# Samples read as the last 128 of 288 columns: full tiles for norms and transposes, and last squares summed in PSUM

## The chip, the cores and the metric

The kernel runs on one core of a Trainium2 chip. The metric is the device time of one execution in microseconds, as the median of several runs. Inputs lie in the chip's memory, in float32, and so do the outputs.

## The reference, cut to what matters

One inference step of a two-layer decoder over a prompt of 512 tokens and 8 samples of 8 tokens each, with 1024 features: a recurrent layer (with an FFN), one shared key/value projection, an attention layer (with an FFN) and a last norm.

```python
def rms_norm(x, g):
    y = xf * lax.rsqrt(jnp.mean(xf * xf, axis=-1, keepdims=True) + EPS)
    return y * g

for l in range(DEPTH):                                   # 2
    h = modulate(rms_norm(x, norm_g[l, 0]), sh1, sc1)
    if l < N_A_LAYERS:  out = recurrent_block(h, ...)
    else:               out = sliding_sink_attention(q, k_all, v_all, ...) @ attn_w_o
    x = x + g1 * out
    h = modulate(rms_norm(x, norm_g[l, 1]), sh2, sc2)
    x = x + g2 * swiglu(h, ffn_w_in[l], ffn_w_out[l])
    if l == 0:
        kv = modulate(rms_norm(x, kv_norm_g), kv_shift, kv_scale) @ w_kv   # k is rotated
y = rms_norm(x, final_g)
```

The outputs are y for prompt and samples, states of the recurrent layer, and the windows of keys and values with the new ones at their end (`sample_k`, `sample_v`, `prompt_k`, `prompt_v`).

## The kernel before

**Layout.** Tokens are split into two halves h = 0 and 1. A half has 288 columns (`HC`): 256 of the prompt (`HP`) and 32 of four samples. `x[h]` holds the residual stream as 128 features by 8 chunks (`KC`) by 288 tokens, so features lie on partitions and tokens along the free axis. A product of a layer is a chain of matmuls with 128x128 weights and 288 columns moving. Every operand is split into a high and a low part, so each weight block takes three matmuls.

**Order.** The code calls `T` (PE), `V` (DVE), `S` (ACT), `G` (POOL) and `Q` (SP, which issues DMAs); these only record operations, all at line 447 of the profile. A planner (`Recorder.schedule`) then lays all operations out by priority (the place where they were recorded, less what `early(n)` takes off), by estimated costs and by free buffers, and each engine runs its own list in that order. A changed number of operations or buffers therefore moves others too.

**Norms.** While a layer's last product is drained, `residual` adds each chunk to x and `square` adds its square to `acc[h]`. `stats` sums `acc` over the features with matmuls that have `acc` as weights and a column of ones moving: one for each block of tokens in `TOK`, 128, 128 and 32 of them, so that each token's sum lies on a partition. A DVE operation scales them, and `spread` takes the power -1/2 on POOL and turns the columns back into a row that is repeated on all partitions, by three PE transposes; the third has 32 rows. This happens for both halves at three places in the middle (two `norm_f`, one `after_ffn0`) and, spread alone, twice at the start (`x_half`).

**Attention.** `evac_v` transposes the new values (their 32 sample columns into 32 rows) and writes them out; `attn_sample` attends over cache and new tokens, `pn` being the 32 rows of probabilities for the new ones, and `k_out` transposes the new sample keys, once for each of two head groups and each half.

**The last stage.** `out` walks over the chunks m of the last product, all of half 0 ahead of half 1. For each it calls `residual` and `final_chunk`, which transposes the chunk of x back to tokens on partitions (128, 128 and 32 rows) and multiplies by the final gain. After m = 7 comes `final_norm`: square of chunk 7 into its own buffer, sums of `acc` and of that square, three scalings, three powers, then each of three row blocks is scaled in two parts (DVE and ACT) and written by two DMAs.

In profile rows, `mm` and `ada` are PSUM banks, `wh` weight parts, `h` the high and low operands or, in the last stage, the output rows, `small` the column of ones, `ident` the identity, `tst` the columns of sums, and `sl`, `ta`, `tb`, `td` work buffers.

Of the kernel before, what the change touches and what calls it, by code (L numbers as in the profile page):

```python
# [473 lines left out]
def trunk_kernel(ctx, tc, a):  # L474
# [702 lines left out]
    def ffn(l, g, after):  # L1177
# [173 lines left out]
        def out(k, m, h):  # L1351
# [6 lines left out]
            residual(h, o, m, g, last)  # L1358
# [129 lines left out]
    def evac_v(gp):  # L1488
        def f(h, o):
# [6 lines left out]
            T.transpose(t[0:32, 2 * P : 3 * P], u.f[:, HP:HC], ident[:])  # L1496
# [7 lines left out]
            V.tensor_copy(vs[h][0:32, gs], t[0:32, 2 * P : 3 * P])  # L1504
            for b in range(4):
                Q.dma_start(
                    a["sample_v"][4 * h + b, P - NT : P].rearrange("t g d -> t (g d)")[:, gs],
                    vs[h][b * NT : (b + 1) * NT, gs],
# [137 lines left out]
    def attn_sample(bl):  # L1646
        def run(h):
# [17 lines left out]
            pn = KT[1].f[0:32, 0:512].rearrange("p (g b n) -> p g b n", g=2, b=4)  # L1665
# [15 lines left out]
            def second():  # L1681
                t = aux()
                T.transpose(t[:, 0:P], e.f[:, 0:P], ident[:])
                T.transpose(t[0:32, P : 2 * P], e.f[:, P:W], ident[:])
# [3 lines left out]
                V.tensor_copy(pn[:, :, bl, :], t[0:32, P : 2 * P].rearrange("p (g n) -> p g n", g=2))  # L1688
# [8 lines left out]
                for gp in range(2):  # L1697
                    T.matmul(av[:, 256 * gp : 256 * gp + 256], vs[h][0:32, gp * P : (gp + 1) * P], pn[:, gp].rearrange("p b n -> p (b n)"), start=False, stop=True, skip_group_check=True)
# [26 lines left out]

    def k_out(h):
        for gp in range(2):
            t = aux()
            T.transpose(t[0:32, 0:P], A["nk"][:, gp, h, :], ident[:])
            ko_ = sl()  # L1730
            ko = ko_.f[0:32, 0:128]
            S.copy(ko, t[0:32, 0:P])
            for b in range(4):
                Q.dma_start(
                    a["sample_k"][4 * h + b, P - NT : P].rearrange("t g d -> t (g d)")[:, gp * P : (gp + 1) * P],
                    ko[b * NT : (b + 1) * NT, :],
                )
            ko_.done()
            if h == 1:
                T.transpose(t[:, P : 2 * P], KT[0].f[:, gp * 512 + 3 * P : gp * 512 + 4 * P], ident[:])  # L1740
                po = A["out"][gp]
                S.copy(po, t[:, P : 2 * P])
                Q.dma_start(a["prompt_k"][0].rearrange("t g d -> t (g d)")[:, gp * P : (gp + 1) * P], po)

# [42 lines left out]
    def final_chunk(h, c):  # L1787
# [10 lines left out]
        for i, n in enumerate((P, P, 32)):  # L1798
            V.tensor_tensor(yt[h][i][0:n, cs], t[0:n, i * P : (i + 1) * P], gfin[0:n, cs], ALU.mult)

    def final_norm(h):

        w = ta()
        S.activation(w.f[:, 0:HC], x[h][:, KC - 1, :], AF.Square)
        pt = [aux()[0 : ts.stop - ts.start, 0:1] for ts in TOK]
        st, rs = tst[h][:, 0:3], tst[h][:, 3:6]
# [3 lines left out]
        w.done()  # L1810
        for t in range(3):
            n = P if t < 2 else 32
            V.tensor_scalar(st[0:n, t : t + 1], pt[t], 1.0 / D, EPS, ALU.mult, ALU.add)
            G.tensor_tensor(rs[0:n, t : t + 1], st[0:n, t : t + 1], mhalf[0:n, 0:1], ALU.pow)
            for i in range(2):
                cs = slice(512 * i, 512 * i + 512)
                y = yt[h][t][0:n, cs]
                if i:
                    S.activation(y, y, AF.Copy, scale=rs[0:n, t : t + 1])
                else:  # L1820
                    V.tensor_scalar(y, y, rs[0:n, t : t + 1], None, ALU.mult)
                if t < 2:
                    Q.dma_start(a["y_prompt"][0, h * HP + t * P : h * HP + (t + 1) * P, cs], y)
                else:
                    Q.dma_start(a["y_sample"][4 * h : 4 * h + 4].rearrange("b t d -> (b t) d")[:, cs], y)
# [4 lines left out]
    def x_half(h):  # L1830
        st = tst[h]
        for t in ((4, 0, 1), (2, 3))[h]:
# [9 lines left out]
            if t == 4:  # L1842
                V.tensor_scalar(tst[0][0:32, 2:3], y[0:32], 1.0 / D, EPS, ALU.mult, ALU.add)
                V.tensor_scalar(tst[1][32:64, 2:3], y[32:64], 1.0 / D, EPS, ALU.mult, ALU.add)
# [157 lines left out]
```

## Time and profile before

| | |
|---|---|
| runs | 1262.38 us median of 3 (1261.91 to 1264.16) |
| profiled execution | 1263.01 us, of which 1261.2 us are the span of its instructions |
| PE busy | 1237.8 us (98%), 9532 matmul records |
| DVE, ACT, POOL busy | 920.3, 663.1, 252.7 us |
| DMA | 165.38 MB, 131 GB/s over the span |
| chain that ended last | PE 86%, DVE 6%, ACT 4%, DMA 2%, POOL 1% |
| PE in the first 60 us, in 670 to 815 us, in the last 10 us | 49.15, 141.69, 2.52 us busy |

A matmul overlaps the next, so busy time of PE is near the span wherever its instructions follow each other; what one of them costs is seen in the distance between starts or ends of groups. A row of the timeline has its start, its length, engine, operation, `out<-in`, the shape of the weight tile (`128*32` is one with 32 columns, `32*128` one with 32 rows) and how many records it merges; in brackets stands how long the engine was idle before it and what ended that. A row of a group has busy time and mean duration in ns.

### The profile page before, as it was taken

Reading aid. Unit: us, or ns where it says so; the run is one execution under the profiler, and the core shown is the slowest. Engines: PE = TensorE matmul, PEld = TensorE weight load, DVE = VectorE, ACT = ScalarE, POOL = GpSimd, SP = SyncE. Lnnn points to the kernel's source line nnn. Section 1 sums busy time; section 2 is a strip of 40 time slices with the busy share of each in tenths; the row PEclk is TensorE's granted clock in tenths of the full one; section 3 lists DMA queues with packets and bytes.
Section 4 is the critical chain, followed back from the end, with each engine's and each line's share of the span. In section 5 each row is a group of like instructions: output and inputs, shape, how many; then the busy total and the mean of one; then the engine's idle time right before and its main releaser. Section 6 shows DMA issues by size and latency. Waiting matters only on the chain.

```text
span 1261.2 us, 25276 instructions
## 1 busy us (share of the span) xinstructions
PE 1237.8 (98%) x9532; PEld 1166.9 (93%) x9532; DVE 920.3 (73%) x2283; ACT 663.1 (53%) x1498; POOL 252.7 (20%) x542
## 2 busy tenths in 40 slices
PE   7999999999999999999999999999999999999997
PEld 5798999899899899989998997999999999999997
DVE  6998784795577468656778887558957865875776
ACT  4788973764255335514567678538523542552442
POOL 3456351101100010011024335100011011001011
PEclk8999999999999999999999999999999999999999
DMA  9955554535456655464513220332342232332322
GB/s 306 318 179 188 188 177 151 170 86 171 140 152 191 185 167 184 156 194 137 167 33 75 68 60 27 111 97 97 85 133 68 84 110 76 90 100 80 100 69 76
DMA packets 219755, 165.38 MB, mean 131 GB/s; under 512 B 23629, under 2 KB 204841, under 8 KB 219602
## 3 DMA queue, kind: packets, MB, share of 16 engines
q1 hardware_dynamic: 219186, 163.45, 43.0%
q8 instruction: 75, 1.23, 0.4%
q0 software_dynamic: 448, 0.32, 0.1%
q14 instruction: 46, 0.38, 0.1%
HBM read 160.85 MB, written 4.87 MB: 131 GB/s over the span
## 4 chain that ended last, share of the span: by engine, by line
PE 86%; DVE 6%; ACT 4%; DMA 2%; POOL 1%; issue 1%; SPq 0%; ACTq 0%; DVEq 0%
PE mm L447 82%; PE ada L447 4%; DVE wh L447 1%; DVE ta L447 1%; ACT tb L447 1%; DVE sl L447 1%; ACT ta L447 1%; DVE tb L447 1%; ACT h L447 1%; DMA raw<-in_rnn_w_in_dram 1%; ACT wh L447 1%; POOL h L447 1%; DMA reg<-in_ada_w_dram 1%; ACT sl L447 1%; DMA reg<-in_x_prompt_dram 1%
## 5 line engine op out<-in xcount | busy, mean ns | idle before, releaser
L447 PE MATMUL mm<-h,wh 128*128 128x288 f32 x4128 | 596.2, 298 | 3.8 <-ACT h L447 1.8
L447 PEld LDWEIGHTS mm<-h,wh 128*128 128x128 f32 x4128 | 560.5, 188 | 23.2 <-issue 11.3
L447 PE MATMUL mm<-sl,wh 128*128 128x288 f32 x3218 | 460.6, 296 | 0.4 <-ACT sl L447 0.3
L447 ACT CAST wh<-raw 128x512 fp32r<-128x512 f32 (+2 forms) x380 | 269.1, 721 | 345.7 <-PE mm L447 208.9
L447 PEld LDWEIGHTS mm<-sl,wh 128*128 128x128 f32 x3218 | 436.6, 188 | 9.0 <-issue 5.9
L447 DVE TENSOR_TENSOR wh<-raw,wh 128x512 fp32r<-128x512 f32 (+2 forms) x380 | 310.2, 828 | 59.3 <-ACT wh L447 57.0
L447 DVE SCALAR_TENSOR_TENSOR x<-mm,mods,x 128x256 f32<-128x256 f32 x160 | 77.0, 482 | 136.1 <-PE mm L447 136.0
L447 POOL TENSOR_TENSOR td<-td,td 128x288 f32<-128x288 f32 x38 | 35.5, 934 | 475.8 <-ACT td L447 467.7
L447 POOL TENSOR_TENSOR x<-x,ta 128x32 f32<-128x32 f32 x152 | 55.3, 364 | 331.1 <-DVE ta L447 325.9
L447 PE MATMUL mm<-tb,wh 128*128 128x288 f32 (+1 forms) x488 | 88.5, 296 | 0.4 <-ACT td L447 0.4
L447 PEld LDWEIGHTS mm<-tb,wh 128*128 128x128 f32 x488 | 72.4, 188 | 1.9 <-DVE sl L447 0.8
L447 ACT COPY td<-mm 128x288 f32<-128x288 f32 (+2 forms) x140 | 49.0, 364 | 37.7 <-DVE mm L447 18.0
L447 DVE TENSOR_TENSOR raw<-raw,raw 128x512 f32<-128x512 f32 x76 | 61.4, 808 | 0.9
L447 PE MATMUL mm<-ta,wh 128*128 128x288 f32 (+1 forms) x254 | 56.1, 298 | 0.0
L447 ACT ACTIVATE ta<-x 128x288 f32<-128x288 f32 x56 | 24.8, 444 | 55.6 <-POOL x L447 52.4
L447 DVE TENSOR_TENSOR raw<-raw 128x512 f32<-128x512 f32 x76 | 52.2, 688 | 1.1
L447 DVE TENSOR_TENSOR td<-mm,td 128x288 f32<-128x288 f32 x76 | 34.5, 454 | 23.4 <-PE mm L447 23.3
L447 PE MATMUL ada<-reg,cz 128*32 128x512 f32 (+1 forms) x448 | 49.5, 553 | 0.0
L447 PEld LDWEIGHTS mm<-ta,wh 128*128 128x128 f32 x254 | 41.7, 188 | 1.8 <-ACT wh L447 0.8
L447 ACT ACTIVATE ta<-ta,stat 128x128 f32<-128x128 f32 (+2 forms) x72 | 32.3, 471 | 18.5 <-DVE stat L447 17.7
L447 DVE TENSOR_TENSOR acc<-acc,ta 128x288 f32<-128x288 f32 x54 | 25.1, 464 | 12.4 <-ACT ta L447 12.4
L447 ACT CAST sl<-ta 128x288 fp32r<-128x288 f32 x54 | 23.0, 431 | 18.5 <-DVE ta L447 18.5
(202 smaller groups left out, 1197.9 us busy)
## 6 DMA issues: line engine op xcount, KB each, us to landing
raw<-in_ffn_w_in_dram SPq DMA_DIRECT2D x88, 512.0 KB
reg<-in_ada_w_dram SPq DMA_DIRECT2D x80, 512.0 KB
raw<-in_ffn_w_out_dram SPq DMA_DIRECT2D x48, 384.0 KB
raw<-in_rnn_w_in_dram SPq DMA_DIRECT2D x16, 512.0 KB
reg<-in_kv_ada_w_dram SPq DMA_DIRECT2D x16, 512.0 KB
wh<-in_ada_w_dram SPq DMA_DIRECT2D x24, 256.0 KB
raw<-in_rnn_w_out_dram SPq DMA_DIRECT2D x8, 512.0 KB
raw<-in_ffn_w_out_dram SPq DMA_DIRECT2D x8, 512.0 KB
```

The source lines that it names most:

```text
L447: self.rec.add(eng, lambda: getattr(obj, name)(*map(real, args), **{k: real(v) for k, v in kw.items()}), cost, outs, ins, func, lat, port, ...
```

## The change

The samples' block of tokens is read as the last 128 of the 288 columns (160 to 287), whose last 32 are the samples. So its sums, spreads and transposes are full 128x128 tiles, and the samples lie on rows 96 to 127 (`TAIL`) of what they give; `spread` writes the wide third block first and lets the other two overwrite what isn't wanted. Rows 0 to 95 of those results aren't read. In `k_out` one transpose takes both halves and head groups together, and one ACT copy.

In the last stage the second-last chunk's square (`late_square`) is kept in its own buffer and not added to `acc`; PE sums three sources into one bank, and one scaling serves all three columns. The residual of chunk 7 and the final norm get an earlier priority (`early(60)`), powers come as two operations instead of three, and each row block is written by one DMA instead of two.

```diff
-    TOK = [slice(0, P), slice(P, 2 * P), slice(2 * P, HC)]
+    late_square = [None, None]
+    TOK, TAIL = [slice(0, P), slice(P, 2 * P), slice(HC - P, HC)], slice(P - 32, P)
     def stats(h):
         for t, ts in enumerate(TOK):
-            T.matmul(pt[0 : ts.stop - ts.start, t : t + 1], acc[h][:, ts], ones, start=True, stop=True)
-        V.tensor_scalar(st[:, 0:2], pt[:, 0:2], 1.0 / D, EPS, ALU.mult, ALU.add)
-        V.tensor_scalar(st[0:32, 2:3], pt[0:32, 2:3], 1.0 / D, EPS, ALU.mult, ALU.add)
+            T.matmul(pt[:, t : t + 1], acc[h][:, ts], ones, start=True, stop=True)
+        V.tensor_scalar(st, pt[:, 0:3], 1.0 / D, EPS, ALU.mult, ALU.add)
-    def spread(h, r0=0):
+    def spread(h, r0=P - 32):
-        for t, ts in enumerate(TOK):
-            r = slice(r0, r0 + 32) if t == 2 else ALL
-            T.transpose(o[:, ts], rs[r, t : t + 1].to_broadcast([r.stop - r.start, P]), ident[r, r])
+        for t, n0 in ((2, HP - r0), (0, 0), (1, P)):
+            T.transpose(o[:, n0 : n0 + P], rs[:, t : t + 1].to_broadcast([P, P]), ident[:])
...
     def residual(h, o, c, g, last):
-        if last and (g != L1 + G2 or c < KC - 1):
+        if last and g == L1 + G2 and c == KC - 2:
+            late_square[h] = s = ta()
+            S.activation(s.f[:, 0:HC], x[h][:, c, :], AF.Square)
+        elif last and (g != L1 + G2 or c < KC - 1):
             square(h, c)
...
         def out(k, m, h):
-            residual(h, o, m, g, last)
+            with early(60 if last and l == 1 and m == KC - 1 else 0):
+                residual(h, o, m, g, last)
...
     def evac_v(gp):
-            T.transpose(t[0:32, 2 * P : 3 * P], u.f[:, HP:HC], ident[:])
+            T.transpose(t[:, 2 * P : 3 * P], u.f[:, TOK[2]], ident[:])
-            V.tensor_copy(vs[h][0:32, gs], t[0:32, 2 * P : 3 * P])
+            V.tensor_copy(vs[h][TAIL, gs], t[TAIL, 2 * P : 3 * P])
     def attn_sample(bl):
-                T.transpose(t[0:32, P : 2 * P], e.f[:, P:W], ident[:])
+                T.transpose(t[:, P : 2 * P], e.f[:, W - P : W], ident[:])
-                    T.matmul(av[:, 256 * gp : 256 * gp + 256], vs[h][0:32, ...], ...)
+                    T.matmul(av[:, 256 * gp : 256 * gp + 256], vs[h][TAIL, ...], ...)
     def k_out(h):
+        if h == 0:
+            t = aux()
+            T.transpose(t[:, 0:P], A["nk"].rearrange("p g h n -> p (g h n)"), ident[:])
+            nkT.append(sl())
+            S.copy(nkT[0].f[:, 0:P], t[:, 0:P])
         for gp in range(2):
-            T.transpose(t[0:32, 0:P], A["nk"][:, gp, h, :], ident[:])
-            S.copy(ko, t[0:32, 0:P])
...
     def final_chunk(h, c):
-        T.transpose(t[0:32, 2 * P : 3 * P], x[h][:, c, HP:HC], ident[:])
+        T.transpose(t[:, 2 * P : 3 * P], x[h][:, c, TOK[2]], ident[:])
     def final_norm(h):
-        for i in range(2):
-            for o, ts in zip(pt, TOK):
-                T.matmul(o, (acc[h], w.f)[i][:, ts], ones, start=i == 0, stop=i == 1)
+        with early(60):
+            sums = (acc[h], late_square[h].f, w.f)
+            for i, y in enumerate(sums):
+                for t, ts in enumerate(TOK):
+                    T.matmul(pt[:, t : t + 1], y[:, ts], ones, start=i + t == 0, stop=i == 2, skip_group_check=True)
+            V.tensor_scalar(st, pt[:, 0:3], 1.0 / D, EPS, ALU.mult, ALU.add)
+            G.tensor_tensor(rs[:, 0:1], st[:, 0:1], mhalf[:, 0:1], ALU.pow)
+            G.tensor_tensor(rs[:, 1:3], st[:, 1:3], mhalf[:, 1:3], ALU.pow)
-                    Q.dma_start(a["y_prompt"][0, h * HP + t * P : h * HP + (t + 1) * P, cs], y)
+                Q.dma_start(a["y_prompt"][0, h * HP + t * P : h * HP + (t + 1) * P, :], y)
```

The order that the planner makes of it is shown at three places. On PE at the end of the kernel, half 1, before (mm_16161 is the product of chunk 7, its last rows; mm_16181 and mm_16192 hold chunks 6 and 7 transposed; a row without a count is one instruction):

```order
L447 MATMUL mm_16161<-sl_15749,wh_15701 128x288
L447 MATMUL mm_16161<-sl_15757,wh_15701 128x288
L447 MATMUL mm_16161<-sl_15749,wh_15717 128x288
L447 MATMUL mm_16181<-ident,x_65 128x128 x2
L447 MATMUL mm_16181<-ident,x_65 32x128
L447 MATMUL mm_16192<-ident,x_65 128x128 x2
L447 MATMUL mm_16198<-small,acc_70 128x1
L447 MATMUL mm_16201<-small,acc_70 128x1
L447 MATMUL mm_16205<-small,acc_70 32x1
L447 MATMUL mm_16192<-ident,x_65 32x128
L447 MATMUL mm_16198<-small,ta_16203 128x1
```

And of the change (mm_16136 is the product of chunk 7, mm_16151 and mm_16180 hold chunks 6 and 7 transposed, ta_16158 is the late square, ta_16183 that of chunk 7):

```order
L447 MATMUL mm_16151<-ident,x_65 128x128 x2
L447 MATMUL mm_16136<-sl_15633,wh_15685 128x288
L447 MATMUL mm_16136<-sl_15645,wh_15685 128x288
L447 MATMUL mm_16160<-small,acc_70 128x1 x3
L447 MATMUL mm_16160<-small,ta_16158 128x1 x3
L447 MATMUL mm_16151<-ident,x_65 128x128
L447 MATMUL mm_16136<-sl_15633,wh_15701 128x288
L447 MATMUL mm_16136<-sl_15733,wh_15685 128x288
L447 MATMUL mm_16136<-sl_15741,wh_15685 128x288
L447 MATMUL mm_16136<-sl_15733,wh_15701 128x288
L447 MATMUL mm_16180<-ident,x_65 128x128 x3
L447 MATMUL mm_16160<-small,ta_16183 128x1 x3
```

The sums of acc and of the late square, and chunk 6's transposes, moved ahead of the last four products of chunk 7; before, they stood behind all of them.

On PE at the end of the attention stage, before (mm_10588 <- wh,reg is the product of the sample probabilities with the new values, h_10346 the second half's operand, mm_10843 its first product):

```order
L447 MATMUL mm_10588<-wh_9720,reg_7879 128x256 x2
L447 MATMUL mm_10792<-h_10033,wh_10583 128x288
L447 MATMUL mm_10792<-h_10033,wh_10533 128x288 x2
L447 MATMUL mm_10792<-h_10033,wh_10583 128x288
L447 MATMUL mm_10792<-h_10033,wh_10533 128x288 x2
L447 MATMUL mm_10792<-h_10033,wh_10583 128x288
L447 MATMUL mm_10792<-h_10033,wh_10533 128x288 x2
L447 MATMUL mm_10792<-h_10033,wh_10583 128x288
L447 MATMUL mm_10843<-h_10346,wh_9780 128x288
```

And of the change (mm_10566 is the sample product, h_10342 the second half's operand):

```order
L447 MATMUL mm_10566<-wh_9716,reg_7877 128x256 x2
L447 MATMUL mm_10782<-h_10029,wh_10474 128x288
L447 MATMUL mm_10782<-h_10029,wh_10433 128x288 x2
L447 MATMUL mm_10782<-h_10029,wh_10474 128x288
L447 MATMUL mm_10835<-h_10029,wh_10601 128x288 x2
L447 MATMUL mm_10841<-h_10342,wh_9776 128x288
```

Four products fewer stand between the sample product and the first one that reads the second half's operand.

On ACT in the middle of the attention stage, before (sl_10423 and sl_10427 take the transposed k of half 0, ta_10342 and tb_10232 a sample's transposed key cache, ta_10416 is a softmax row):

```order
L447 COPY sl_10423<-mm_10377 32x128
L447 COPY sl_10427<-mm_10389 32x128
L447 CAST h_10033<-ada_10408 128x256
L447 ACTIVATE ta_10416,stat_95<-ta_10416,stat_95 128x256
L447 COPY ta_10342<-mm_10441 128x128
L447 COPY tb_10232<-mm_10441 128x128
```

And of the change:

```order
L447 COPY sl_10421<-mm_10373 128x128
L447 CAST h_10029<-ada_10404 128x256
L447 CAST wh_10433<-raw_9650 128x1024
L447 COPY ta_10338<-mm_10436 128x128
L447 COPY tb_10228<-mm_10436 128x128
L447 ACTIVATE ta_10411,stat_95<-ta_10411,stat_95 128x256
```

A weight conversion (wh_10433), which stood some fifteen rows further down, moved ahead of the key copies and of the softmax.

More of the change, by code (lines that the diff above doesn't have):

```diff
@@ L1697, in second @@
                 for gp in range(2):
-                    T.matmul(av[:, 256 * gp : 256 * gp + 256], vs[h][0:32, gp * P : (gp + 1) * P], pn[:, gp].rearrange("p b n -> p (b n)"), start=False, stop=True, skip_group_check=True)
+                    T.matmul(av[:, 256 * gp : 256 * gp + 256], vs[h][TAIL, gp * P : (gp + 1) * P], pn[:, gp].rearrange("p b n -> p (b n)"), start=False, stop=True, skip_group_check=True)
                 for j, r in enumerate(HALF):
@@ L1724, in attn_open @@
         part(h)
+    nkT = []
     def k_out(h):
-        for gp in range(2):
-            t = aux()
-            T.transpose(t[0:32, 0:P], A["nk"][:, gp, h, :], ident[:])
-            ko_ = sl()
-            ko = ko_.f[0:32, 0:128]
-            S.copy(ko, t[0:32, 0:P])
+        if h == 0:
[3 more added lines that the diff above has]
+            S.copy(nkT[0].f[:, 0:P], t[:, 0:P])
+        for gp in range(2):
             for b in range(4):
+                r = 32 * (2 * gp + h) + b * NT
                 Q.dma_start(
                     a["sample_k"][4 * h + b, P - NT : P].rearrange("t g d -> t (g d)")[:, gp * P : (gp + 1) * P],
-                    ko[b * NT : (b + 1) * NT, :],
+                    nkT[0].f[r : r + NT, 0:P],
                 )
-            ko_.done()
             if h == 1:
+                t = aux()
                 T.transpose(t[:, P : 2 * P], KT[0].f[:, gp * 512 + 3 * P : gp * 512 + 4 * P], ident[:])
@@ L1743, in k_out @@
                 Q.dma_start(a["prompt_k"][0].rearrange("t g d -> t (g d)")[:, gp * P : (gp + 1) * P], po)
+        if h == 1:
+            nkT[0].done()
     def attn_fin(h):
@@ L1794, in final_chunk @@
             T.transpose(t[:, b * P : (b + 1) * P], x[h][:, c, b * P : (b + 1) * P], ident[:])
-        T.transpose(t[0:32, 2 * P : 3 * P], x[h][:, c, HP:HC], ident[:])
+        T.transpose(t[:, 2 * P : 3 * P], x[h][:, c, TOK[2]], ident[:])
         cs = slice(c * P, (c + 1) * P)
         gfin = Y[h][:, 3 * D : 4 * D]
-        for i, n in enumerate((P, P, 32)):
-            V.tensor_tensor(yt[h][i][0:n, cs], t[0:n, i * P : (i + 1) * P], gfin[0:n, cs], ALU.mult)
+        for i, r in enumerate((ALL, ALL, TAIL)):
+            V.tensor_tensor(yt[h][i][r, cs], t[r, i * P : (i + 1) * P], gfin[r, cs], ALU.mult)
@@ L1801, in final_norm @@
     def final_norm(h):
[L1803 to L1806, printed above, removed]
-        for i in range(2):
-            for o, ts in zip(pt, TOK):
-                T.matmul(o, (acc[h], w.f)[i][:, ts], ones, start=i == 0, stop=i == 1)
-        w.done()
+        with early(60):
+            w = ta()
+            S.activation(w.f[:, 0:HC], x[h][:, KC - 1, :], AF.Square)
+            pt = aux()
+            st, rs = tst[h][:, 0:3], tst[h][:, 3:6]
+            sums = (acc[h], late_square[h].f, w.f)
+            for i, y in enumerate(sums):
+                for t, ts in enumerate(TOK):
+                    T.matmul(pt[:, t : t + 1], y[:, ts], ones, start=i + t == 0, stop=i == 2, skip_group_check=True)
+            late_square[h].done()
+            w.done()
+            V.tensor_scalar(st, pt[:, 0:3], 1.0 / D, EPS, ALU.mult, ALU.add)
+            G.tensor_tensor(rs[:, 0:1], st[:, 0:1], mhalf[:, 0:1], ALU.pow)
+            G.tensor_tensor(rs[:, 1:3], st[:, 1:3], mhalf[:, 1:3], ALU.pow)
@@ L1811, in final_norm @@
         for t in range(3):
-            n = P if t < 2 else 32
-            V.tensor_scalar(st[0:n, t : t + 1], pt[t], 1.0 / D, EPS, ALU.mult, ALU.add)
-            G.tensor_tensor(rs[0:n, t : t + 1], st[0:n, t : t + 1], mhalf[0:n, 0:1], ALU.pow)
+            r = ALL if t < 2 else TAIL
             for i in range(2):
-                cs = slice(512 * i, 512 * i + 512)
-                y = yt[h][t][0:n, cs]
+                y = yt[h][t][r, 512 * i : 512 * i + 512]
                 if i:
-                    S.activation(y, y, AF.Copy, scale=rs[0:n, t : t + 1])
+                    S.activation(y, y, AF.Copy, scale=rs[r, t : t + 1])
@@ L1843, in x_half @@
                 V.tensor_scalar(tst[0][0:32, 2:3], y[0:32], 1.0 / D, EPS, ALU.mult, ALU.add)
-                V.tensor_scalar(tst[1][32:64, 2:3], y[32:64], 1.0 / D, EPS, ALU.mult, ALU.add)
+                V.tensor_scalar(y, y, 1.0 / D, EPS, ALU.mult, ALU.add)
         V.tensor_scalar(st[:, 0:2], st[:, 0:2], 1.0 / D, EPS, ALU.mult, ALU.add)
```

15 lines of the change are left out of this document (8 added, 7 removed).

## The prediction

> **What bounds the kernel now.** I read the page's first part, then the window table, to see whether TensorE (PE) is the limit everywhere, and then PE's timeline at the four kinds of place that the change touches, since only start times there give the price of one instruction.
>
> ```profile
> PE 1237.8 (98%) x9532; PEld 1166.9 (93%) x9532; DVE 920.3 (73%) x2283; ACT 663.1 (53%) x1498; POOL 252.7 (20%) x542
> ...
> 1190.00:1220.00 30.00, 30.00 (x229) 30.00 (x228) 22.86 (x38) 16.94 (x36) 2.66 (x3) 1.00 0.30 100
> ```
>
> PE is busy 98% of the span, and a stretch of plain products runs 229 instructions in 30.00 us: 0.131 us each, at the full granted clock (1.00). A product's own duration is longer, as they overlap; what an inserted instruction costs is therefore read between the ends of the product groups around it, less 0.131 for each product. Outside the attention stage and the last 10 us, time that PE loses or gains is time of the kernel.
>
> **The spreads.** Three transposes turn a norm's per-token column into rows; the third has 32 rows of input. PE's timeline at one of them:
>
> ```profile
> 644.40 0.97 PE L447 MATMUL mm<-sl,wh 128*128 128x288 f32 x6
> 645.21 0.55 PE L447 MATMUL mm<-ident,tst 128*128 128x128 f32 x3
> 645.69 0.94 PE L447 MATMUL mm<-sl,wh 128*128 128x288 f32 x5
> ```
>
> The product groups end at 645.37 and 646.63: 1.26 us, less five products (0.655), leaves 0.605 for three transposes. What full and 32-column transposes cost is read in the last stage, where both stand between products:
>
> ```profile
> 1242.33 0.38 PE L447 MATMUL mm<-sl,wh 128*128 128x288 f32 x1
> 1242.55 0.38 PE L447 MATMUL mm<-ident,x 128*128 128x128 f32 x2
> 1242.69 0.51 PE L447 MATMUL mm<-sl,wh 128*128 128x288 f32 x2
> 1243.03 0.27 PE L447 MATMUL mm<-ident,x 128*32 128x128 f32 x1
> 1243.06 0.51 PE L447 MATMUL mm<-sl,wh 128*128 128x288 f32 x2
> ...
> L447 PEld LDWEIGHTS mm<-ident,x 128*128 128x128 f32 x32 | 4.2, 140 | 0.4 <-DVE x L447 0.3
> L447 PEld LDWEIGHTS mm<-ident,x 128*32 128x32 f32 x16 | 1.5, 95 | 0.2 <-POOL x L447 0.2
> ```
>
> Two full ones: ends 1242.71 to 1243.20, 0.49 - 0.262 = 0.228, so 0.114 each. One of 32 columns: ends 1243.20 to 1243.57, 0.37 - 0.262 = 0.108. In a spread the 32-row one therefore costs 0.605 - 0.228 = 0.377 and becomes a full one of 0.114: 0.263 saved, at six spreads between products 1.58 us. The two spreads of the start are left at nothing: there PE waits for loads anyway; had they been in its path, they would give 2 x 0.263 = 0.5 more.
>
> **The transposes of 32 columns** (16 of the last stage, 12 of v and the sample probabilities) become full ones: 0.108 against 0.114, nothing. Ends of the unknown here: the 45 ns by which a full weight load is longer (140 against 95), paid 28 times, is +1.26; the drop that the spread's third shows, 28 times, is -7.4. I take 0, because the in-stream row is the operation itself.
>
> The Trainium skill, page "TensorEngine Tiling (Array Packing)", section Key Properties, says that changing the tiling mode drains TensorE. The trace agrees for the 32-row transpose (0.377 against 0.114) and not for the 32-column one (0.108); by the rule the latter would be worth the 7.4 us, the first rival. The same skill, "TensorE: Matmul & The Clock Gate", section "LDWEIGHTS (loading the stationary operand)", gives a load as columns / 1.2 ns, which speaks against the change: an estimate by that page is 80 ns more for each full load, 2.2 us over 28. The trace has 45 ns, and none of it between the products.
>
> **The sums of squares.** Each matmul onto the ones column stands as two records (x6 for three column blocks). The last stage's first half has every form, full and of 32 columns:
>
> ```profile
> 1235.27 0.38 PE L447 MATMUL mm<-sl,wh 128*128 128x288 f32 x1
> ...
> 1235.48 0.56 PE L447 MATMUL mm<-small,acc 128*128 128x1 f32 x4
> ...
> 1235.91 0.51 PE L447 MATMUL mm<-sl,wh 128*128 128x288 f32 x2
> ...
> 1236.10 0.19 DVE L447 TENSOR_TENSOR x<-x,ta 128x32 f32<-128x32 f32 x1
> 1236.33 0.44 ACT L447 ACTIVATE ta<-x 128x288 f32<-128x288 f32 x1 [1.66 <-DVE x L447]
> ...
> 1236.35 0.22 PE L447 MATMUL mm<-small,acc 128*32 128x1 f32 x2
> ...
> 1236.50 0.40 PE L447 MATMUL mm<-sl,wh 128*128 128x288 f32 x1
> ...
> 1236.76 0.64 PE L447 MATMUL mm<-sl,wh 128*128 128x288 f32 x3
> ...
> 1237.24 0.65 PE L447 MATMUL mm<-small,ta 128*128 128x1 f32 x6
> ...
> 1237.82 0.93 PE L447 MATMUL mm<-sl,wh 128*128 128x288 f32 x5
> ```
>
> Four full records: ends 1235.65 to 1236.42, 0.77 - 0.262 = 0.508 (0.127 each). A lone pair of 32 columns: 1236.42 to 1236.90, 0.48 - 0.131 = 0.349. Six records, the last two of 32 columns: 1237.40 to 1238.75, 1.35 - 0.655 = 0.695 (0.116 each). Six full ones then cost 0.70 to 0.76, so at the six middle norms the wider sums are worth nothing (between -0.2 and +0.4 over all).
>
> In the last stage there are now three sources instead of two, since the second-last square is no longer added by DVE. First half: before 0.508 + 0.349 + 0.695 = 1.55; now 18 records at 0.116 to 0.127 = 2.09 to 2.29. They stand between products, with no wait: +0.63. The DVE addition that goes is worth nothing, as DVE is not the limit there.
>
> **The tail.** The second half ends the kernel:
>
> ```profile
> 1249.20 1.96 PE L447 MATMUL mm<-sl,wh 128*128 128x288 f32 x13
> ...
> 1251.20 0.48 DVE L447 SCALAR_TENSOR_TENSOR x<-mm,mods,x 128x256 f32<-128x256 f32 x1 [0.27 <-PE mm L447]
> ...
> 1251.60 0.18 DVE L447 TENSOR_TENSOR ta<-mm,mods 128x32 f32<-128x32 f32 x1
> ...
> 1252.92 0.44 ACT L447 ACTIVATE ta<-x 128x288 f32<-128x288 f32 x1 [1.19 <-DVE x L447]
> ...
> 1253.42 0.76 PE L447 MATMUL mm<-small,ta 128*128 128x1 f32 x6
> ...
> 1254.08 0.28 DVE L447 TENSOR_SCALAR tst<-mm 128x1 f32<-128x1 f32 x3
> 1254.29 1.66 POOL L447 TENSOR_TENSOR tst<-tst,small 128x1 f32<-128x1 f32 x3 [3.03 <-DVE tst L447]
> 1254.88 1.58 DVE L447 TENSOR_SCALAR h<-h,tst 128x512 f32<-128x512 f32 x3 [0.51 <-POOL tst L447]
> ...
> 1255.39 1.82 SPq L447 DMA_DIRECT2D out_y_prompt_dram<-h  x4
> ...
> L447 ACT ACTIVATE h<-h,tst x6: 706/708/723, 1238.5 to 1256.1; 128x512 f32<-128x512 f32 x4, 32x512 f32<-32x512 f32 x2
> ...
> 1256.20:1259.50 3.30, 0.00 (x0) 0.00 (x0) 0.26 (x1) 0.62 (x2) 0.00 (x0) 0.50 1.01 354
> ```
>
> Before, the last product ends at 1251.16 and scaling begins at 1254.88, 3.72 later. Two things happen to this. First, the new order puts the sums of acc and of the late square, 12 records, ahead of the last four products, and chunk 6's three transposes too, which before followed the last product: 12 x 0.116 to 0.127 (1.45) + 3 x 0.114 = 1.79 us by which the last product ends later. They used to be covered by the residual's chain on DVE; now nothing covers them. Second, that chain gets shorter, as residual and norm are taken early. From the last product's end at 1251.16: x 1251.20 to 1251.68, ta until 1251.78, x<-x,ta directly behind (0.19, as at 1236.10, and some 0.03 of gap) until 1252.00, square from 1252.04 to 1252.48, six sums (0.56 for four, so 0.78) from 1252.54 to 1253.32, one scale of the sums for three (from 1253.37), the power 0.21 after its start (1254.08 to 1254.29 before), scaling another 0.59 later: 1254.17 instead of 1254.88, -0.71. The late square is no wait: its chain, from its product's end, takes about as long as the last one's (1251.16 to 1252.48, 1.3 us), and eight products (1.05) and the sums of acc (0.7) lie between.
>
> After scaling, the DMA engines are full (1.01 of them, 354 GB/s over 3.30 us), and the bytes stay. The first transfer is issued when ACT's half is done (0.72) rather than DVE's (0.51): +0.22. Three issues instead of six save nothing, because the engines and not SP set the end. Tail: 1.79 - 0.71 + 0.22 = +1.30; ends +0.8 (sums at the pace of a bare record, larger rows moving faster) and +1.7.
>
> **The attention stage.** One transpose in place of four k transposes and one ACT copy in place of four save up to 3 x 0.114 = 0.34. Against it stands the new order. At the end of the stage, the sample columns of h15, which the first product of the second half needs, come from this:
>
> ```profile
> 785.65 0.51 ACT L447 ACTIVATE ta<-ta,stat 128x256 f32<-128x256 f32 x1 [0.58 <-POOL ta L447]
> ...
> 808.42 1.13 PE L447 MATMUL mm<-wh,reg 32*128 32x256 f32 x4
> 809.48 2.19 PE L447 MATMUL mm<-h,wh 128*128 128x288 f32 x12
> ...
> 810.68 0.41 ACT L447 CAST h<-sl 128x256 fp32r<-128x256 f32 x1 [0.35 <-DVE sl L447]
> ...
> 810.66 1.23 DVE L447 TENSOR_TENSOR wh<-raw,wh 128x1024 fp32r<-128x1024 f32 x1
> 811.81 0.42 DVE L447 TENSOR_TENSOR h<-sl,h 128x256 fp32r<-128x256 f32 x1
> ...
> L447 ACT CAST wh<-raw 128x1024 fp32r<-128x1024 f32 x66 | 68.9, 1047 | 35.4 <-PE mm L447 34.3 <-DMA raw<-in_rnn_w_in_dram 0.8 <-DMA raw<-in_ffn_w_out_dram 0.2
> ```
>
> The cast ends at 811.09, and ten products separate the sample product from its first reader now, six afterwards: 4 x 0.131 = 0.52 more waiting; its low half (until 812.23, behind a weight conversion) is then read some 0.4 sooner. So +0.9 here, -0.34 for the transposes: I take +0.5, ends -0.5 (the earlier conversions pay back) and +2.1. SP has a load piece of attn_w_o ahead of the k outputs; nobody waits for those.
>
> **The sum**: -1.58 + 0.63 + 1.30 + 0.5 = +0.85 us. The profiled execution took 1263.01 (span 1261.2) and would take 1263.86; it lies 0.63 above the median of the runs, 1262.38, so the forecast is 1263.2, no change that a measurement of this kernel can tell (0.2%, 2.5 us: 1259.9 to 1264.9).
>
> **Rivals.**
> - Faster: leaving the 32-column form saves what leaving the 32-row form does, 28 x 0.263 = 7.4: 1255.8. For it: the pair of 32-column sums cost 0.349. Against: the transposes' own 0.108. 7%.
> - Slower: in the attention stage a weight conversion (ACT 1.05, DVE 1.23) now stands ahead of the key copies and softmax of the first half's last chunk, and PE's first product of attn_w_o waits for that chain. If both fall on it, +2.28: 1265.5. It decides from some 1.7 us of wait upward. For it: that product waits already. Against: ACT stands idle 0.58 between two softmax steps there (785.65). 14%.
> - The spreads' saving is swallowed, since in the attention stage PE waits for others: +1.58, 1264.8. Against: the stages after it run PE without gaps. 11%.
> - The full weight loads come through, 28 x 45 ns: 1264.5, 5% (by that page's figure 1265.4).
>
> **How the numbers follow.** My case has 63%; 1263.2 is its value, 1261.2 to 1265.2 its own range by the ends above. Faster 7% (the first rival); slower 16% (three quarters of the second, a third of the third, half of the fourth); the rest is same. The range 1260.6 to 1265.6 leaves out the first rival and the top of the second.
>
> **What would show it.** Spreads: three full transposes at about 0.34 between products, not 0.6. Last stage: 32-column groups gone without the products moving closer; the last product ending near 1253 rather than 1251.2; from there to scaling 3.0 instead of 3.7. Attention: a longer gap before the first h15 product. I am wrong if the product groups around single transposes of the last stage have moved together by 0.2, or if the last four products do not stand behind the 12 sums.

## The result and the profile after

The changed kernel took 1269.17 us (median of 4 runs, 1267.06 to 1269.68) against 1263.04 (4 runs, 1261.91 to 1264.16): 1.0045 of the time before, 95% interval 1.0032 to 1.0059. It is slower by some 5.7 us; the forecast was 1263.2, no measurable change, with a range of 1260.6 to 1265.6. The profiled execution is the shortest of the four, 1267.06 us with a span of 1265.2, 4.0 above that of before. So the two profiles show 4.0 of the 5.7 us; the rest lies in runs without a profile.

The page and the stretch of plain products, as they were shown of before. PE has 9 records more and is as busy as ever; plain products run at the same pace, 228 in 30 us:

```profile
PE 1240.0 (98%) x9541; PEld 1169.5 (92%) x9541; DVE 923.2 (73%) x2271; ACT 663.4 (52%) x1495; POOL 250.6 (20%) x540
...
1190.00:1220.00 30.00, 30.00 (x228) 30.00 (x228) 22.69 (x40) 16.80 (x35) 2.65 (x3) 1.00 0.32 105
```

Where the time went is seen when both traces are cut at the first transpose of the last stage: 1222.58 us before, 1221.75 after, with 168 products still to come in both. Up to there the changed kernel is 0.83 us ahead. From there to the end it takes 43.47 us instead of 38.66. The window of that stage (columns: length, then busy time and instructions of PE, weight loads, DVE, ACT, POOL), before:

```profile
1222.58:1261.24 38.66, 31.14 (x242) 29.66 (x239) 26.10 (x104) 10.89 (x22) 7.10 (x20) 0.93 0.18 62
```

and after:

```profile
1221.75:1265.22 43.47, 33.80 (x254) 31.52 (x252) 28.79 (x98) 11.32 (x22) 5.93 (x18) 0.91 0.15 55
```

DVE has six instructions fewer and is busy 2.7 us longer. That is the surprise, and the timeline of PE and DVE shows it. One chunk of the last stage before: DVE's three multiplications by the gain, then the next chunk's residual, and the transposes that read it:

```profile
1226.40 1.98 PE L447 MATMUL mm<-sl,wh 128*128 128x288 f32 x13
...
1226.95 0.67 DVE L447 TENSOR_TENSOR h<-mm,h 128x128 f32<-128x128 f32 x3
...
1227.54 0.46 DVE L447 SCALAR_TENSOR_TENSOR x<-mm,mods,x 128x256 f32<-128x256 f32 x1
...
1228.22 0.38 PE L447 MATMUL mm<-ident,x 128*128 128x128 f32 x2
1228.35 0.52 PE L447 MATMUL mm<-sl,wh 128*128 128x288 f32 x2
```

and the same chunk after:

```profile
1225.80 1.95 PE L447 MATMUL mm<-sl,wh 128*128 128x288 f32 x13
...
1226.48 0.79 DVE L447 TENSOR_TENSOR h<-mm,h 128x128 f32<-128x128 f32 x3
...
1227.31 0.48 DVE L447 SCALAR_TENSOR_TENSOR x<-mm,mods,x 128x256 f32<-128x256 f32 x1
...
1227.85 0.44 PE L447 MATMUL mm<-ident,x 128*128 128x128 f32 x2
1228.04 0.51 PE L447 MATMUL mm<-sl,wh 128*128 128x288 f32 x2
```

The order is the same. Before, the residual starts 0.59 us behind the first multiplication (1226.95 to 1227.54), after 0.83 (1226.48 to 1227.31). The third multiplication, on 32 rows, overlapped its neighbours while those were rows 0 to 31; on rows 96 to 127 it overlaps neither. (A row `x3` merges the three and gives the shape of the first alone.) PE's transposes wait for that residual: between the products' ends, less the two products behind them, they took 0.23 us before (1228.38 to 1228.87, less 0.26) and take 0.54 now (1227.75 to 1228.55). Over the stage the transposes take 7.00 us of PE (45 of them) instead of 4.84 (44). The wait itself stands at the weight loads of these transposes (the last column is idle time and what ended it), before, of the 128-column ones, and after:

```profile
L447 PEld LDWEIGHTS mm<-ident,x 128*128 128x128 f32 x30 | 4.0, 140 | 0.0
L447 PEld LDWEIGHTS mm<-ident,x 128*128 128x128 f32 x45 | 5.8, 142 | 2.1 <-DVE x L447 1.9
```

The spread that was shown of before, after:

```profile
643.93 1.57 PE L447 MATMUL mm<-sl,wh 128*128 128x288 f32 x10
645.34 0.49 PE L447 MATMUL mm<-ident,tst 128*128 128x128 f32 x3
645.59 2.63 PE L447 MATMUL mm<-sl,wh 128*128 128x288 f32 x18
```

From 645.50 to 648.22 stand 18 products (2.36 us) and 0.36 us of transposes, where it was 0.605. This is the spread that gains most; at the other five, read with the next five products, it is 0.38 to 0.49. And the tail:

```profile
1252.24 0.51 PE L447 MATMUL mm<-sl,wh 128*128 128x288 f32 x2
1252.66 0.80 PE L447 MATMUL mm<-small,acc 128*128 128x1 f32 x6
1253.32 0.81 PE L447 MATMUL mm<-small,ta 128*128 128x1 f32 x6
1253.99 0.31 PE L447 MATMUL mm<-ident,x 128*128 128x128 f32 x1
1254.05 0.77 PE L447 MATMUL mm<-sl,wh 128*128 128x288 f32 x4
...
1254.33 0.80 DVE L447 TENSOR_TENSOR h<-mm,h 128x128 f32<-128x128 f32 x3 [1.11 <-PE mm L447]
1255.16 0.48 DVE L447 SCALAR_TENSOR_TENSOR x<-mm,mods,x 128x256 f32<-128x256 f32 x1
...
1258.20 0.49 DVE L447 TENSOR_SCALAR h<-h,tst 128x512 f32<-128x512 f32 x1 [0.67 <-POOL tst L447]
...
1258.94 1.12 SPq L447 DMA_DIRECT2D out_y_prompt_dram<-h  x2
```

The last product ends at 1254.82. Its residual does not start there but at 1255.16, behind three slow multiplications.

The longer gap that was to show at the first product of the second half in the attention stage is there too, 0.59 us where before PE had none:

```profile
812.42 1.81 PE L447 MATMUL mm<-h,wh 128*128 128x288 f32 x9 [0.59 <-ACT h L447]
```

### The profile page after: what moved, and what is told of

Its sections match the earlier page's. It is cut to its first block, busy times and chain, and to the rows that moved or that the text cites. A ratio compares the mean times of both kernels' runs of the same rounds, so it can differ in the third digit from the quotient of the medians.

```text
span 1265.2 us, 25266 instructions
## 1 busy us (share of the span) xinstructions
PE 1240.0 (98%) x9541; PEld 1169.5 (92%) x9541; DVE 923.2 (73%) x2271; ACT 663.4 (52%) x1495; POOL 250.6 (20%) x540
## 3 DMA queue, kind: packets, MB, share of 16 engines
q8 instruction: 75, 1.23, 0.4%
## 4 chain that ended last, share of the span: by engine, by line
PE 86%; DVE 6%; ACT 3%; issue 1%; DMA 1%; POOL 1%; SPq 0%; ACTq 0%; POOLq 0%; DVEq 0%
PE mm L447 82%; PE ada L447 5%; DVE wh L447 1%; DVE sl L447 1%; ACT tb L447 1%; DMA reg<-in_ada_w_dram 1%; DVE h L447 1%; DVE ta L447 1%; DVE tb L447 1%; ACT ta L447 1%; ACT h L447 1%; SPq L447 0%; DVE acc L447 0%; DMA raw<-in_attn_w_q_dram 0%; DVE stat L447 0%
```

## The experiments

All times beside 1262.6 to 1262.9 for the kernel before on the same chips. The stage's length is read as above, from the first transpose of the last stage to the end of the span; where two of the versions below share its code it agrees within 0.1 us, far better than the times, so each experiment has both. The one profile of the kernel before has 38.66 us, the six others with its last stage 38.41 to 38.51.

**The final multiplication on all rows.**

```diff
-        for i, r in enumerate((ALL, ALL, TAIL)):
+        for i, r in enumerate((ALL, ALL, ALL)):
```

> The changed kernel, with the third multiplication of each final chunk done on all 128 rows of the transposed tile instead of rows 96 to 127; no other instruction and no order differs. Theory 1 (late VectorE): in the last stage the multiplication on rows 96 to 127 overlaps neither the one before it nor the instruction behind it (starts 0.296 and 0.31 to 0.33 us apart, where they were 0.197 before), 0.23 us for each of 16 chunks, so the residuals come late and PE waits for x at the transposes (they took 7.00 us of PE between 1221.75 and 1254.82, before 4.84). On all rows the spacing goes back to 0.20 and 2 to 3 us go: median 1266 to 1267, transposes near 5.0 us. Theory 2 (the order written for the last stage, sums and norm taken early, is what costs): the spacing may change, the time does not, 1269 within 0.8.

1266.94 us, 1.0028 [1.0017, 1.0040]. The last stage takes 40.86 us, 2.6 less than the changed kernel's, and the transposes 4.97. The rows:

```profile
1229.22 0.68 DVE L447 TENSOR_TENSOR h<-mm,h 128x128 f32<-128x128 f32 x3
1229.81 0.47 DVE L447 SCALAR_TENSOR_TENSOR x<-mm,mods,x 128x256 f32<-128x256 f32 x1
```

0.59 us again: four times as many rows cost no time, and the overlap is back. The wait of the weight loads is gone:

```profile
L447 PEld LDWEIGHTS mm<-ident,x 128*128 128x128 f32 x45 | 6.1, 142 | 0.0
```

No order differs, so theory 1 stands for 2.6 of the stage's 4.8 us; theory 2 fails as the whole cause.

**Rows 64 to 127**, to see what it is about rows 96 to 127.

```diff
-        for i, r in enumerate((ALL, ALL, TAIL)):
+        for i, r in enumerate((ALL, ALL, slice(64, P))):
```

> The changed kernel with the third multiplication of each final chunk on rows 64 to 127 instead of 96 to 127, orders unchanged. Theory 1a (what holds a VectorE instruction is that it starts at another group of 32 partitions than its neighbours): starts stay 0.29 to 0.31 us behind the second multiplication, and the next instruction 0.31 to 0.33 behind this one; the last stage, from the first final transpose to the end, stays 43 us or more. Theory 1b (only the last quarter of the partitions is slow, or 32 rows are): spacing 0.20 and a last stage near 40.9 us.

One run, 1268.88 us; the stage takes 44.04 us.

```profile
1227.71 0.79 DVE L447 TENSOR_TENSOR h<-mm,h 128x128 f32<-128x128 f32 x3
1228.53 0.48 DVE L447 SCALAR_TENSOR_TENSOR x<-mm,mods,x 128x256 f32<-128x256 f32 x1
```

0.82 us from the first multiplication to the residual, with 64 rows that begin elsewhere: theory 1a. What matters is at which partition the instruction begins, not how many rows it has nor that they are the last ones. All its operands begin there at once, and no run has two neighbours that both begin at 96; so these runs do not tell which operand counts, nor whether the comparison is with the neighbours, as theory 1a has it, or with partition 0. The Trainium skill, page "VectorE: DVE Perf Modes", section "Two Vector instructions with no wait between them", gives a model of this with the neighbours: an instruction of which an operand starts in another group of 32 partitions than the last one did in the same memory is held until every earlier one has finished. The trace agrees, at 64 and at 96: the third multiplication starts 0.01 to 0.03 us after the second has ended.

**The last stage as before**, all else changed (final transposes of 32 columns, two sources, six output DMAs, no early priority). The core of the edit:

```diff
-        T.transpose(t[:, 2 * P : 3 * P], x[h][:, c, TOK[2]], ident[:])
+        T.transpose(t[0:32, 2 * P : 3 * P], x[h][:, c, HP:HC], ident[:])
...
-        for i, r in enumerate((ALL, ALL, TAIL)):
-            V.tensor_tensor(yt[h][i][r, cs], t[r, i * P : (i + 1) * P], gfin[r, cs], ALU.mult)
+        for i, n in enumerate((P, P, 32)):
+            V.tensor_tensor(yt[h][i][0:n, cs], t[0:n, i * P : (i + 1) * P], gfin[0:n, cs], ALU.mult)
```

> The changed kernel with the last stage (final transposes, late square, final sums and scaling, six output DMAs) as it was before; the norms inside the program and the attention stage stay changed. Both theories: the whole loss is in the last stage, so this is faster than before by the spreads' 1.1 to 1.6 us and gives back up to 0.5 in the attention stage: 1261.5 to 1262.4 against 1263.0 before. If the loss lies elsewhere (in runs that were not profiled, two of which were 2 us longer than the profiled one): 1264 or more.

1264.80 us, 1.0011 [1.0002, 1.0020]; the stage takes 38.41 us. So the last stage is most of the loss but not all of it: by the ratio 1.4 us stay, where 0.6 to 1.5 below before were expected. Both theories missed this.

**No early priority.**

```diff
-            with early(60 if last and l == 1 and m == KC - 1 else 0):
-                residual(h, o, m, g, last)
+            residual(h, o, m, g, last)
...
-        with early(60):
+        with early(0):
```

> The changed kernel with the priority of the last residual and of the final norm taken away, so that the last four products are free to go ahead of the 12 sums again. Theory 1 (late VectorE): the waits for x stay; what comes back is the tail's own term, 1.8 less 0.7: 1268.1, and PE's transposes of the last stage still take about 7 us. Theory 2 (the order): most of the loss goes, 1264 to 1265.

1268.55 us, 1.0043 [1.0030, 1.0055]; the stage takes 42.64 us, 0.8 less than with the priority, where theory 1 has 1.1. Early priority is worth no more than that, and theory 2 is out.

**The norms alone.** The kernel before with `TOK`, `stats` and `spread` changed, final sums still over 128, 128 and 32 columns. Against before:

```diff
-            T.matmul(pt[0 : ts.stop - ts.start, t : t + 1], acc[h][:, ts], ones, start=True, stop=True)
+            T.matmul(pt[:, t : t + 1], acc[h][:, ts], ones, start=True, stop=True)
...
-            T.transpose(o[:, ts], rs[r, t : t + 1].to_broadcast([r.stop - r.start, P]), ident[r, r])
+            T.transpose(o[:, n0 : n0 + P], rs[:, t : t + 1].to_broadcast([P, P]), ident[:])
```

> The kernel before with only the norms inside the program changed: sums over three full column blocks, spreads of three full transposes. By the starts in the changed kernel's trace a spread now costs 0.30 to 0.38 us instead of 0.61, 1.1 to 1.6 us over six: 1261.4 to 1261.9 against 1263.0. The rival, that this is swallowed by waits behind it: 1263.0 within 0.4. The difference to the run with the attention stage changed too is that stage's own price: 0 to +0.5 expected.

1262.77 us, 0.9994 [0.9985, 1.0003]: a saving of 0.8 us by the point value, anything from 1.9 to -0.4 by the interval. In the traces of all changed versions a spread costs PE 0.10 to 0.27 us less than before at each of the six places. What of that reaches the time is less clear. Between the spread at 845 us and the last stage, with two spreads, this run is faster by 0.8 (376.95 to 376.16 us), but the two spreads account for 0.29 of it. Most of the rest builds up little by little among plain products between 1042 and 1179 us, where both kernels run the same instructions. All thirteen profiles with the changed norms take 376.15 to 376.31, but there is only one of before, so it stays open whether that part belongs to the change. Between the sums at 218 us and the spread at 664 it is not faster (445.32 to 445.68), though three spreads lie there. PE waits elsewhere instead, in part for weight conversions. Before, and in this run:

```profile
654.42 6.85 PE L447 MATMUL mm<-h,wh 128*128 128x288 f32 x43
...
657.18 2.01 PE L447 MATMUL mm<-h,wh 128*128 128x288 f32 x11 [0.15 <-ACT wh L447]
659.46 2.40 PE L447 MATMUL mm<-h,wh 128*128 128x288 f32 x16 [0.26 <-DVE wh L447]
```

So the attention stage's part of the change costs 1.0011 less 0.9994, some 2 us by point values. Three runs take it apart: the k output alone, the rest (v and probabilities) alone, and both with copies on all rows and the last stage as before. The core of the first edit:

```diff
+            T.transpose(t[:, 0:P], A["nk"].rearrange("p g h n -> p (g h n)"), ident[:])
...
-            T.transpose(t[0:32, 0:P], A["nk"][:, gp, h, :], ident[:])
```

> The kernel before, with the changed norms inside the program and the changed k output (one transpose and one ACT copy in place of four); v, the sample probabilities and the last stage as before. It has the changed kernel's order of the attention stage. Theory K (the order that the k output brings): a VectorE conversion of 1.2 us stands ahead of the chain that the first attn_w_o product waits for, PE idles about 1.4 us there and in most runs loses another 1.5 us or so to a granted clock of 0.5 behind it: about 1264.8, as with the whole attention stage changed, against 1262.8 for the norms alone. Theory V (VectorE copies of the sample rows, now on rows 96 to 127, no longer overlap their neighbours): this run has none of them, 1262.8 or a little less.

1262.93 us, 0.9998 [0.9989, 1.0006]. Against the norms alone, the second has, beside the full transposes of v and the probabilities:

```diff
-            V.tensor_copy(vs[h][0:32, gs], t[0:32, 2 * P : 3 * P])
+            V.tensor_copy(vs[h][TAIL, gs], t[TAIL, 2 * P : 3 * P])
...
-                V.tensor_copy(pn[:, :, bl, :], t[0:32, P : 2 * P].rearrange("p (g n) -> p g n", g=2))
+                V.tensor_copy(pn[:, :, bl, :], t[TAIL, P : 2 * P].rearrange("p (g n) -> p g n", g=2))
```

> The kernel before, with the changed norms inside the program and the changed v and sample probabilities (full transposes, VectorE copies from rows 96 to 127); the k output and the last stage as before. It keeps the order that the attention stage had before. Theory K: 1262.8, as with the norms alone, plus at most 0.5. Theory V: about 1264.8, with starts of the 32-row copies 0.3 us behind the one ahead of them instead of 0.2.

1263.31 us, 1.0004 [0.9995, 1.0012]. And the third, against the changed kernel:

```diff
-            V.tensor_copy(vs[h][TAIL, gs], t[TAIL, 2 * P : 3 * P])
+            V.tensor_copy(vs[h][:, gs], t[:, 2 * P : 3 * P])
...
-                V.tensor_copy(pn[:, :, bl, :], t[TAIL, P : 2 * P].rearrange("p (g n) -> p g n", g=2))
+                V.tensor_copy(pn[:, :, bl, :], t[:, P : 2 * P].rearrange("p (g n) -> p g n", g=2))
```

> The changed kernel with the last stage as before and with the VectorE copies of v's and the probabilities' sample rows done on all 128 rows instead of rows 96 to 127; PE's order in the attention stage stays that of the changed kernel. Theory K: still about 1264.8, PE still idle 1.2 us or more ahead of the first attn_w_o product. Theory V: 1262.5 to 1263, that idle time mostly gone.

1262.85 us, 1.0000 [0.9991, 1.0009]. Neither theory holds alone: the intervals overlap, and the point values give about 0.5 us to the k output's order, 1.2 to the copies on rows 96 to 127, and 1.4 back with all rows. PE still idles 1.23 us ahead of the first attn_w_o product in the last of the three, as theory K has it, but its time is that of theory V. DVE's copies with v on rows 96 to 127:

```profile
785.15 0.27 DVE L447 COPY td<-mm 128x128 f32<-128x128 f32 x1
785.46 0.30 DVE L447 COPY wh<-mm 32x128 f32<-32x128 f32 x1
785.78 0.29 DVE L447 COPY td<-mm 128x128 f32<-128x128 f32 x1
786.11 0.30 DVE L447 COPY wh<-mm 32x128 f32<-32x128 f32 x1
```

and in the last run of this section, on all rows and in the same DVE order:

```profile
782.77 0.27 DVE L447 COPY td<-mm 128x128 f32<-128x128 f32 x1
782.97 0.28 DVE L447 COPY wh<-mm 128x128 f32<-128x128 f32 x1
783.17 0.27 DVE L447 COPY td<-mm 128x128 f32<-128x128 f32 x1
783.36 0.27 DVE L447 COPY wh<-mm 128x128 f32<-128x128 f32 x1
```

0.31 to 0.33 us from start to start against 0.20. In profiles in which the clock stays up (below), the copies on all rows shorten the stage from the spread at 664 to the sums at 844 us by 0.28 us with the changed order (179.89 to 179.61) and by 0.66 with the old one (180.60 to 179.94). With all rows and the changed order two profiles agree (179.61 and 179.63); each of the other three lengths is from one profile. The rest of the 1.2 to 1.4 is within the scatter of the times.

The k output's part looks different. The first attn_w_o product before, and the rows ahead of it in the changed kernel's trace:

```profile
788.24 2.06 PE L447 MATMUL mm<-h,wh 128*128 128x288 f32 x12 [0.23 <-ACT h L447]
...
785.55 1.21 DVE L447 TENSOR_TENSOR wh<-raw,wh 128x1024 fp32r<-128x1024 f32 x1
...
786.69 0.44 PE L447 MATMUL mm<-ident,wh 128*128 128x128 f32 x2
...
786.79 0.28 DVE L447 COPY sl<-mm 64x128 f32<-64x128 f32 x1
...
788.12 0.39 ACT L447 CAST h<-sl 128x256 fp32r<-128x256 f32 x1
...
788.56 1.93 PE L447 MATMUL mm<-h,wh 128*128 128x288 f32 x11 [1.43 <-ACT h L447]
```

A weight conversion stands ahead of the chain of the first attn_w_o product, which waits 1.43 us. By itself that costs nothing: from the spread at 663.7 to the next sums at 843.6 us the changed kernel's profile takes 179.89 us and that of before 179.88, since the same work was done earlier. But what comes behind the gap differs from run to run. The granted clock (third number from the end) in the changed kernel's profile:

```profile
789.00:790.00 1.00, 1.00 (x8) 0.98 (x8) 1.00 (x7) 0.91 (x2) 0.80 (x2) 1.00 0.91 266
790.00:791.00 1.00, 1.00 (x11) 1.00 (x10) 0.80 (x6) 0.94 (x4) 0.28 (x2) 1.00 0.70 225
```

and in that of the run with the old last stage, behind the same gap of 1.43 us:

```profile
789.00:790.00 1.00, 1.00 (x6) 1.00 (x5) 1.00 (x8) 0.97 (x4) 0.78 (x2) 0.50 0.79 249
790.00:791.00 1.00, 1.00 (x6) 0.98 (x6) 0.36 (x3) 0.62 (x3) 0.00 (x0) 0.50 0.57 182
791.00:792.00 1.00, 1.00 (x6) 1.00 (x5) 0.00 (x0) 0.00 (x0) 0.21 (x1) 0.50 0.69 204
```

At half the clock products start every 0.24 us instead of 0.13, for 3.41 us (788.80 to 792.21); that stage took 181.95 us there, 2.1 more. Of the ten profiles with this order (gap 1.21 to 1.69 us) seven show the drop, of the four with the order of before (no gap over 0.32 us at this place) one. The Trainium skill, page "TensorE: Matmul & The Clock Gate", section "HAM oscillation — how this bites in real kernels", warns of idle gaps over some 3.4 us; here drops stand behind gaps of half that. That the gap causes the drop is suggested by these counts and not shown: filling the gap was not tried, and behind waits of 0.6 to 1.3 us at 691 to 696 us, which all fourteen profiles have, no drop follows. The changed kernel's profiled run escaped it, and its three other runs, without a profile, are 1.9 to 2.6 us longer.

**Two sources for the last sums.** All rows in the final multiplication, and

```diff
-            sums = (acc[h], late_square[h].f, w.f)
+            sums = (acc[h], w.f)
```

with the second-last square added to `acc` as before.

> The changed kernel with all rows in the final multiplication, and the second-last square added to acc by VectorE again, so that the last sums have two sources and 12 records instead of three and 18; the early priority stays. By the prediction's prices six records of 0.116 to 0.127 us go from each half, 0.7 + 0.7 = 1.4 us in all: 1265.5 against 1266.9 for the run on all rows with three sources. The rival, that the records are free because something else is waited for (the residual's chain): 1266.9 within 0.6.

1264.82 us, 1.0018 [1.0007, 1.0028], against 1.0028 with three sources; the stage takes 39.35 us instead of 40.86. Predicted 1.4, measured 1.5 by the stage and 1.3 by the ratio: the records are paid in full.

**All rows everywhere.** The edits of the first and of the third attention run together:

```diff
+        for i, r in enumerate((ALL, ALL, ALL)):
...
+            V.tensor_copy(vs[h][:, gs], t[:, 2 * P : 3 * P])
```

> The changed kernel with every VectorE instruction that it put on rows 96 to 127 between full ones (final multiplication, v, probabilities) done on all 128 rows; nothing else differs, orders included. If these are all that the prediction left out, what remains are its own terms: by their prices +0.85 us over before, with the spreads at the 0.13 us each that the traces now show +1.7, and with the last stage at the +2.2 that the run on all rows in the last stage shows, +2.0: 1264.3 to 1265.3 against 1262.8, where the changed kernel took 1.0045 of before (+5.7). If something else is missing as well: 1267 or more.

1265.48 us, 1.0029 [1.0017, 1.0040], by the median 0.2 above what was expected and by the ratio (3.7 us over before) more; the stage takes 40.89 us, as with the final multiplication alone. The ratio is no better than there, though the attention copies are mended. Six of its seven runs have a mean granted clock of 0.990 to 0.993, while most of before's have 0.994 to 0.997. So the clock may have taken back what the copies gave, which runs without a profile cannot show; its profiled run, without the drop, has a span of 1261.4 us.

The same, with two sources:

```diff
-            sums = (acc[h], late_square[h].f, w.f)
+            sums = (acc[h], w.f)
```

> The run before this one, with the second-last square added to acc by VectorE again (12 records for each half's sums instead of 18). If the runs' differences add up, this takes another 1.25 to 1.5 us away: 1263.0 to 1264.0, at before's time within 0.1%. The rival, that the two gains overlap since both shorten the same waits: 1264.5.

1263.64 us, 1.0006 [0.9997, 1.0015]; the stage takes 39.33 us. By the stage the two gains, 2.6 and 1.6, add up.

**What the runs point to.** The changed norms, full transposes of v and the probabilities with copies on all rows, the old k output and the old last stage; against the run with the norms alone:

```diff
-            T.transpose(t[0:32, 2 * P : 3 * P], u.f[:, HP:HC], ident[:])
+            T.transpose(t[:, 2 * P : 3 * P], u.f[:, TOK[2]], ident[:])
...
-            V.tensor_copy(vs[h][0:32, gs], t[0:32, 2 * P : 3 * P])
+            V.tensor_copy(vs[h][:, gs], t[:, 2 * P : 3 * P])
```

> What the runs point to as the fastest version: the changed norms inside the program, v and the probabilities as full transposes with copies on all rows, and the old k output and last stage. By the run with v on rows 96 to 127 (1.0004) and the one with the norms alone (0.9994) the copies on all rows bring back 1.0: 0.9994, 1262.0 against 1262.8. If the full transposes themselves cost (45 ns for each longer weight load, 12 of them, 0.5 us): 0.9998.

1261.62 us, 0.9989 [0.9980, 0.9997]: faster than both kernels, by about 1.4 us against before (0.4 to 2.5 by the interval). The full transposes cost nothing that shows.

## Why the prediction was wrong

**The step that failed** is the one on the 32-column transposes, "0.108 against 0.114, nothing". Its price for PE was right: 45 full transposes took 4.97 us in the run on all rows, 0.11 each. What had no term at all is the instruction that reads each of them: 16 multiplications and 12 copies on DVE moved from rows 0 to 31 to rows 96 to 127, and each then delays itself and the next by 0.1 us. "DVE is not the limit there" hid it: in the last stage before, the residual of the chunk shown ends at 1228.00 and its transposes start at 1228.22. A chain with 0.2 us to spare does not bear 0.24 more for each chunk. The measured size is 2.6 us in the last stage, shown by the run that changes nothing else, and in the attention stage 0.3 to 0.7 by its length, 1.2 to 1.4 by point values of the times, which is less sure.

**The sums** were right. Wider sums changed PE's time at each middle norm by 0.05 us at most, in every profile that has them. The third source in the last stage was +0.63 for the first half and six of the tail's 12 records, 1.4 together: 1.5 measured.

**The tail** was right in its parts. The 12 sums and the transpose ahead of the last four products take 1.55 us in the rows above (1252.75 to 1254.82, less 0.52), by the prediction 1.45 and 0.11. Without the slow multiplications the last stage is 2.4 us longer than in the kernels with the old one (40.86 to 38.45), against the 1.93 of the terms for sums and tail. From the last product to scaling it is 3.14 us there, and 3.38 in the changed kernel, where 3.0 was forecast: the residual waits for the three multiplications. The first issue comes 0.74 behind scaling, where 0.72 was forecast.

**The spreads** were over-sized: 0.263 each was worked out, 0.10 to 0.27 came, 1.0 us over six instead of 1.58. Three full transposes were priced at 0.34 by one reading between products and take 0.33 to 0.49 in a spread. Part of the rival "swallowed" is true too: what three of them save is not seen at 664 us.

**The attention stage**: the second rival's place was right, a weight conversion ahead of the softmax chain and PE waiting for it, but not its price: the wait cost nothing on balance (179.89 to 179.88 us), and where it costs, it is by the clock behind it. The forecast's gap at the second half's first product came (0.52 more waiting forecast, 0.59 there). That its +0.5 agrees with the point value for the k output is luck as far as the runs go: the interval holds zero, and in profiles without the drop, with copies on all rows, the stage is not longer with the new order (179.61) than with the old one (179.94).

**The narrow-transposes rival** (-7.4) fell as the row said: full transposes moved nothing together.

The sum by the measured parts, point values of the times for all but the last stage: spreads -0.8, sums and tail +2.4, k output +0.5, instructions on other rows 2.6 and 1.2: +5.9, against 5.7 by the ratio. The terms that come from the times are uncertain by about 1 us each, so that this closeness is partly luck; the last stage's 4.8 us are the part that is shown. Left open are how often the clock drops in runs without a profile, how much of the attention stage's part that is, and where exactly the first three spreads' saving goes.

## What to carry to other kernels

When data moves to other partitions, price the instructions that read it there as well as the ones that write it: on DVE, starting at another group of 32 partitions than its neighbours cost an instruction its overlap on both sides, and doing all 128 rows cost nothing. An engine that is busy two thirds of a stage can still set its pace; look at how long its result lies before it is used, not at its share. Where stages repeat closely from run to run, compare their lengths in the traces; the whole time of this kernel scatters by 3 to 4 us and hides half of the effects.

## What the runs showed that was not expected

- A DVE instruction on 32 or 64 rows that starts at partition 96 or 64, between full ones, begins 0.29 to 0.33 us behind its predecessor and holds its successor for 0.31 to 0.33, where 0.20 is the pace at partition 0; on all 128 rows the pace is 0.20 as well.
- After a gap of 1.2 to 1.7 us on PE the granted clock was 0.50 for 3.4 us (once 6.8) in seven of ten profiles. Six of the seven have a profile of the same attention code without the drop beside them; against it the stage was longer by 1.7 to 3.5 us. Once it happened without such a gap.
- Full transposes cost what 32-column ones do (0.11 us each between products), but three of them cost 0.10 to 0.27 us less than two with a 32-row one.
